# Feed-forward by seven block products in place of eight, in two phases with the gated values in DRAM; bias line written from 128 partitions

## The chip, the cores and the metric

The kernel runs on one core of one Trainium2 chip. A core has a tensor engine for matrix products (PE, with its weight loads PEld), a vector engine (DVE), a scalar engine (ACT), a general engine (POOL) and a queue that issues transfers (SP). The tensor engine writes only into PSUM, here eight banks of 128 partitions by 512 float32. The metric is the device time of one execution in microseconds; lower is better.

## The reference, cut to what matters

One decoder layer on 1024 tokens of 1024 features. The first half is a projection, three groups of attention (sliding window with a relative bias, forgetting attention, latent attention), an output projection, a norm and a residual. The second half is the feed-forward:

```
h = rmsnorm(x, ffn_pre_norm)
u = causal_depthwise_conv(h @ w_up, conv_w, conv_b)      # 5632 columns, 3 taps along the tokens
gate, up = split(u, 2)                                   # 2816 each
y = (gelu(gate) * up) @ w_down
x = x + rmsnorm(y, ffn_post_norm)
```

The relative bias that the sliding window needs is a line of 384 values for each of 8 heads; every query row reads it shifted by one, so it is kept in DRAM once for each of 128 rows.

## The kernel before, in words

Everything is float32. A matrix product is taken as three matmuls of rounded parts: high by high, low by high, high by low (`mm3`, lines 154 to 157). The high part is a rounding copy (`copy_hi`), the low part a subtraction (`sub`).

**Feed-forward.** The 5632 columns of `w_up` are 44 tiles of 128: tile i below 22 is gate, tile 22+i is the up column that belongs to it. `up(i, c)` (line 849) computes one tile for one half c of the tokens: 8 blocks of 128 features by three matmuls of 512 columns, 24 matmuls into one PSUM bank. Bias and the last tap are one ACT instruction that reads the bank (line 861); the other two taps are DVE instructions that also read the bank (line 863), with a two-column `edge` kept for the seam of the halves. Then come gelu, the product gate by up, and the two parts `guh` and `gul`, which stay in SBUF. `down(grp, ...)` (line 1000) multiplies a group of three (at last four) finished tiles by their rows of `w_down`: per block of 128 tokens and half of the columns 9 (12) matmuls into one bank, added by DVE into `yacc`. `fsteps2` (line 56) interleaves: six up tiles, one group of down, and so on. In the last group, each block of tokens is normed, added to the residual `x2d` and stored.

**Weights** are loaded and split by `w_ahead` in the order of the list `wkeys`, four ahead for the load and two for the split; an up tile's split is a cast and a subtraction on DVE, a down tile's is on ACT and POOL (`ENG`, line 38).

**Room.** Nearly all tiles of SBUF come from one pool of 43 slots of 4 KB per partition (`S`, line 95). PSUM has three tags: `mm` and `tp` of two banks each, `sc` of two pairs of banks.

**Bias line.** `bias_line` (line 650) is the filler step `BL` of `FORDER`, late in the dense attention: one small matmul, one DVE addition, and one transfer that writes the 8 rows, each repeated 128 times, from 8 partitions to `bd` in DRAM (1.5 MB). `make_bias` (step `MB`) reads it back.

**Order.** Instructions are written in the order of the program; a scheduler then sets the order of each engine's queue. Each engine runs its queue strictly in that order and waits on semaphores; all transfers are issued by SP, in order.

Of the kernel before, what the change touches and what calls it, by code (L numbers as in the profile page):

```python
# [9 lines left out]
F32 = mybir.dt.float32  # L10
# [3 lines left out]
ALU = mybir.AluOpType  # L14
# [14 lines left out]
          "VAa VAb A2a BL SV A1a A1b A0a A0b A3a A3b MB A2b")  # L29
# [14 lines left out]
GROUPS = (3,) * 6 + (4,)  # L44
# [6 lines left out]
       "F13": 12.11}  # L51
REL = {"Q": -0.965, "A0": 0.595, "A1": 0.092, "M10": 2.221, "B0": 1.243, "M11": 0.739, "O1": 2.446, "B1": 1.525,
       "M20": 2.627, "M21": 1.902, "O0": 2.761, "P": 3.706, "X": 1.747}


def fsteps2():

    s = []
    i0 = 0
    for n in GROUPS:  # L60
        i1 = i0 + n
        for i in range(i0 + 1, i1):
            s += [("up", (i,)), ("up", (NC2 + i,))]
        if i1 < NC2:
            s.append(("up", (i1,)))
        s.append(("dn", tuple(range(i0, i1))))
        if i1 < NC2:
            s.append(("up", (NC2 + i1,)))
        i0 = i1
    return s  # L70
# [3 lines left out]
def trunk_kernel(ctx: ExitStack, tc: tile.TileContext, a: dict, out: bass.AP):  # L74
# [11 lines left out]
    def E(k):  # L86
        return {"A": A, "V": V, "G": G}[ENG[k]]
# [7 lines left out]
    def S(name, dt=F32, shape=(P, 1024), tag="s", bufs=None):  # L95
        return slots.tile(list(shape), dt, tag=tag, name=name, bufs=bufs)

    def sm(name, w, dt=F32):
        return small.tile([P, w], dt, tag=f"sm{w}", name=name)

    def bank(name, tag="mm", shape=(P, 512)):
        tag = TAGS.get(name, tag)
        return (ps2 if tag == "sc" else ps1).tile(list(shape), F32, tag=tag, name=name)
# [4 lines left out]
    def load(dst, src):  # L108
        dst = dst.bitcast(F32) if dst.dtype == F32R else dst
        src = src.bitcast(F32) if src.dtype == F32R else src  # L110
        nc.sync.dma_start(out=dst, in_=src)

    def const(name, shape, src, dt=F32):
        t = cst.tile(list(shape), dt, name=name)
        load(t, src)
        return t

    def blk(i, n=P):
        return slice(i * n, (i + 1) * n)
# [24 lines left out]
    def copy_hi(dst, src, eng):  # L144
        if eng is V:
            V.tensor_copy(dst, src)  # L146
        else:
            A.copy(dst, src)  # L148

    def sub(dst, x, hi, eng=None):  # L150

        (eng or G).tensor_tensor(out=dst, in0=x, in1=hi.bitcast(F32), op=ALU.subtract)  # L152
# [26 lines left out]
    wkeys.append((("up", 0), a["w_up"][0], 1024))  # L179
    wkeys.append((("up", NC2), a["w_up"][NC2], 1024))  # L180
    for key, i in fsteps2():
        wkeys += [((key, j), a["w_up" if key == "up" else "w_down"][j], 1024) for j in i]
# [107 lines left out]
    bd = dram.tile([8, P, 384], F32, name="bd")  # L290
    x2d = dram.tile([SEQ, D], F32, name="x2d")

    def step(f, *x):
        return lambda: f(*x)
# [76 lines left out]
    for t in range(6, NT):  # L371
        tg1(t)
        if t == 6:
            triu = S("triu")
            load(triu[:, 0:P], a["triu"])
    identb = const("identb", [P, P], a["identb"], BF16)
# [273 lines left out]
    def bias_line():  # L650
        rb = sm("rb", 8)
        load(rb[0:32], a["rel_bias"])
        ol = S("oh")
        load(ol[0:32, 0:384], a["ohl"])
        ml = S("ml")
        load(ml[0:8, 0:384], a["mline"])
        ps = bank("bps", "tp")
        T.matmul(ps[0:8, 0:384], lhsT=rb[0:32], rhs=ol[0:32, 0:384], start=True, stop=True)
        V.tensor_tensor(out=ml[0:8, 0:384], in0=ps[0:8, 0:384], in1=ml[0:8, 0:384], op=ALU.add)
        load(bd, ml[0:8, 0:384].rearrange("p (o u) -> p o u", o=1).broadcast_to([8, P, 384]))  # L660

    def make_bias():

        base = bd[0:1, 0:1, 0:1]
        for g in range(2):
            bias[g] = S(f"bias{g}", F32, (P, 4, 256))
            load(bias[g], bass.AP(tensor=base.tensor, offset=base.offset + 4 * g * P * 384 + 127,
                                  ap=[[383, P], [P * 384, 4], [1, 256]]))
# [178 lines left out]
    gu, ut = {}, {}  # L847
    edge = cst.tile([P, 2 * NC2, 2], F32, name="edge")

    def up(i, c, alt=False):  # L850

        wh, wl = W(("up", i))
        ps = bank("psv") if alt else banks("psu", (P, 512))
        for k in range(NK):
            mm3(ps, wh[:, blk(k)], wl[:, blk(k)], h2h[c, k // 2][:, k % 2], h2l[c, k // 2][:, k % 2], k == 0, k == NK - 1)
        if c == 0:
            ut[i] = S("u")
        u = ut[i]
        w = cw[:, i]
        b0 = 512 * c  # L860
        A.activation(u[:, b0:b0 + 512], ps, AF.Identity, bias=w[:, 3:4], scale=w[:, 2:3])  # L861
        for d in (1, 2):
            V.scalar_tensor_tensor(out=u[:, b0 + d:b0 + 512], in0=ps[:, 0:512 - d], scalar=w[:, 2 - d:3 - d],  # L863
                                   in1=u[:, b0 + d:b0 + 512], op0=ALU.mult, op1=ALU.add)
        if c == 0:
            V.tensor_copy(edge[:, i], ps[:, 510:512])  # L866
        else:
            for d in (1, 2):
                V.scalar_tensor_tensor(out=u[:, 512:512 + d], in0=edge[:, i, 2 - d:2], scalar=w[:, 2 - d:3 - d],
                                       in1=u[:, 512:512 + d], op0=ALU.mult, op1=ALU.add)  # L870
        halves = i % NC2 == NC2 - 1
        if c == 0 and not halves:
            return
        cs = blk(c, 512) if halves else slice(0, 1024)
        if i < NC2:
            A.activation(u[:, cs], u[:, cs], AF.Gelu_apprx_tanh)
        else:
            if i - NC2 not in gu:
                gu[i - NC2] = (S("guh", F32R), S("gul", F32R))
            gt = ut[i - NC2]  # L880
            hi, lo = gu[i - NC2]
            V.tensor_tensor(out=u[:, cs], in0=gt[:, cs], in1=u[:, cs], op=ALU.mult)  # L882
            copy_hi(hi[:, cs], u[:, cs], E("guh"))
            sub(lo[:, cs], u[:, cs], hi[:, cs], V if halves else G)


    def fill_ct(i, c):
# [3 lines left out]
        if CKV <= i < KF1:  # L891
# [5 lines left out]
              "BL": (0.6, bias_line), "MB": (0.1, make_bias)}  # L897
# [64 lines left out]
    def swa_a(n, g):  # L962
# [6 lines left out]
             **{f"F{c}{j}": step(up, i, c, j % 2 == 1 and c == 1) for c in range(2) for j, i in enumerate(PRE)}}  # L969
    for j in range(8):  # L970
        steps[f"w{j}"] = step(w_ahead, wo_i + min(8, j + 3), wo_i + j + 1)
# [21 lines left out]

    yacc = {}

    def up_tile(i):
        up(i, 0)
        up(i, 1)

    def down(grp, first, final):  # L1000
        w = [W(("dn", i)) for i in grp]
        if final:
            gff = S("gff")
            load(gff, a["post"][1:2, :].broadcast_to([P, D]))
        for t in range(NT):
            ends = (512, 768, 1024) if final and t == NT - 1 else (512, 1024)
            if first:
                yacc[t] = S(f"y{t}")
            y = yacc[t]
            if final:  # L1010
                sq = sm(f"ysq{len(ends)}", len(ends))
                xt = S("x2r")
                load(xt, x2d[blk(t), :])
            for c, e in enumerate(ends):
                hs = slice(ends[c - 1] if c else 0, e)
                ps = bank("psd", "mm" if c % 2 else "tp")[:, 0:hs.stop - hs.start]
                for x, i in enumerate(grp):
                    mm3(ps, gu[i][0][:, blk(t)], gu[i][1][:, blk(t)], w[x][0][:, hs], w[x][1][:, hs],
                        x == 0, x == len(grp) - 1)
                if first:  # L1020
                    A.copy(y[:, hs], ps)
                else:
                    V.tensor_tensor(out=y[:, hs], in0=ps, in1=y[:, hs], op=ALU.add)  # L1023
                if final:
                    square_sum(sq[:, c:c + 1], y[:, hs])
                    (V if t == NT - 1 and c else G).tensor_tensor(out=y[:, hs], in0=y[:, hs], in1=gff[:, hs], op=ALU.mult)
            if final:
                s, r = sm("zs", 1), sm("zr", 1)
                V.tensor_reduce(out=s, in_=sq, axis=AX.X, op=ALU.add)
                rstd(r, s, D)  # L1030
                for hf in range(2):
                    hs = blk(hf, 512)
                    V.scalar_tensor_tensor(out=y[:, hs], in0=y[:, hs], scalar=r, in1=xt[:, hs], op0=ALU.mult, op1=ALU.add)  # L1033
                    if t == NT - 1:
                        load(out[0, blk(t), hs], y[:, hs])
                if t < NT - 1:
                    load(out[0, blk(t), :], y)

    for key, i in fsteps2():
        if key == "dn":  # L1040
            down(i, i[0] == 0, i[-1] == NC2 - 1)
        elif i[0] not in PRE:
            up_tile(i[0])
# [83 lines left out]
```

## Time and profile before

| | us |
|---|---|
| median of three runs | 1297.54 (1295.29 to 1299.85) |
| the profiled execution, own time | 1293.17 |
| its span, first to last instruction | 1291.3 |
| feed-forward's matmuls in the trace | 546 to 1279 |

The profiled execution lies 4.4 us under the median of the runs, and 1.9 us of its time lie outside the span. Of the span PE is busy 94%, DVE 57%, ACT 34%, POOL 26%. A busy PE is one with at least one matmul in its pipeline; the rate at which matmuls follow each other is read from their starts.

### The profile page before, as it was taken

The page shows a single profiled execution, that of the slowest core. Times are in us where ns is not written, and L with a number is a line of the kernel's source. Part 1 is how long each engine was busy: PE and PEld are TensorE (multiplying, and loading weights), DVE is VectorE, ACT ScalarE, POOL GpSimd, SP SyncE. Part 2 cuts the span into 40 slices and gives each one's busy share as a digit, 9 for nine tenths or more (in the row PEclk, how much of TensorE's full clock was granted, in tenths as well). Part 3 has the DMA queues.
Part 4 walks back from the last instruction along what each step waited for, and adds up shares of the span by engine and source line. Part 5 has one row for each costly group of instructions (what it writes and reads, how often), then busy time and mean ns, then how long its engine had stood idle before and what let it go on. Part 6 is the DMA issues. An engine that isn't in the chain of part 4 may idle for free.

```text
span 1291.3 us, 15510 instructions
## 1 busy us (share of the span) xinstructions
PE 1217.1 (94%) x5978; PEld 1009.6 (78%) x5978; DVE 738.7 (57%) x1214; ACT 443.7 (34%) x919; POOL 337.4 (26%) x204
## 2 busy tenths in 40 slices
PE   8999999839987999999999999999999999999996
PEld 6978887728776878887887887888888888888885
DVE  6346757414789888747416437436446536535566
ACT  6325623303577777523322202202302202202232
POOL 2223322132685354101301301301301300300254
PEclk9999999959999999999999999999999999999998
DMA  9443345232921221312011111201201202202142
GB/s 336 152 134 76 85 146 179 32 65 71 259 67 49 66 82 66 115 65 82 17 49 43 56 35 48 65 33 49 66 14 55 63 16 65 66 17 65 47 182 98
DMA packets 46146, 105.85 MB, mean 82 GB/s; under 512 B 4577, under 2 KB 21513, under 8 KB 46073
## 3 DMA queue, kind: packets, MB, share of 16 engines
q1 hardware_dynamic: 46072, 104.87, 26.7%
q8 instruction: 47, 0.77, 0.2%
q14 instruction: 27, 0.21, 0.1%
HBM read 83.49 MB, written 20.32 MB: 80 GB/s over the span
## 4 chain that ended last, share of the span: by engine, by line
PE 49%; DVE 12%; issue 2%; ACT 2%; POOL 1%; DVEq 0%; POOLq 0%; ACTq 0%
PE psu L155 9%; PE psu L157 9%; PE psu L156 8%; PE psd L155 5%; PE psd L157 5%; PE psd L156 5%; DVE wh L146 4%; DVE u L863 2%; PE pso L155 2%; PE pso L157 2%; PE pso L156 2%; DVE wl L152 1%; DVE y L1033 1%; DVE u L882 1%; ACT u L861 1%
## 5 line engine op out<-in xcount | busy, mean ns | idle before, releaser
L155 PE MATMUL psu<-h2h,wh 128*128 128x512 f32 x688 | 269.8, 392 | 6.0 <-DVE edge L866 6.0
L156 PE MATMUL psu<-h2l,wh 128*128 128x512 f32 x688 | 268.6, 390 | 0.0
L157 PE MATMUL psu<-h2h,wl 128*128 128x512 f32 x688 | 268.5, 390 | 0.0
L863 DVE SCALAR_TENSOR_TENSOR u<-psu,cw,u 128x511 f32<-128x511 f32 (+1 forms) x172 | 128.0, 744 | 176.5 <-ACT u L861 175.7
L152 POOL TENSOR_TENSOR gul<-u,guh 128x1024 fp32r<-128x1024 f32 x21 | 57.2, 2725 | 561.9 <-ACT guh L148 561.9
L861 ACT ACTIVATE u<-psu,cw 128x512 f32<-128x512 f32 x86 | 67.1, 780 | 377.5 <-PE psu L157 227.2
L155 PEld LDWEIGHTS psu<-h2h,wh 128*128 128x128 f32 x688 | 129.6, 188 | 37.6 <-issue 11.1
L157 PEld LDWEIGHTS psu<-h2h,wl 128*128 128x128 f32 x688 | 129.4, 188 | 26.8
L156 PEld LDWEIGHTS psu<-h2l,wh 128*128 128x128 f32 x688 | 129.6, 188 | 26.4
L152 POOL TENSOR_TENSOR wl<-wraw,wh 128x1024 fp32r<-128x1024 f32 (+1 forms) x47 | 110.8, 2370 | 114.0 <-issue 38.5
L156 PE MATMUL psd<-wl,guh 128*128 128x512 f32 (+1 forms) x356 | 137.6, 387 | 0.0
L157 PE MATMUL psd<-wh,gul 128*128 128x512 f32 (+1 forms) x356 | 137.6, 387 | 0.0
L155 PE MATMUL psd<-wh,guh 128*128 128x512 f32 (+1 forms) x356 | 133.7, 387 | 0.0
L1023 DVE TENSOR_TENSOR y<-psd,y 128x512 f32<-128x512 f32 (+1 forms) x97 | 64.6, 682 | 103.6 <-PE psd L157 103.6
L155 PE MATMUL psct<-hTh,wh 128*128 128x512 f32 x176 | 70.8, 402 | 25.6 <-DVE ct L275 25.6
L146 DVE CAST wh<-wraw 128x1024 fp32r<-128x1024 f32 (+2 forms) x65 | 78.8, 1212 | 26.3 <-PE psu L157 13.7
L156 PEld LDWEIGHTS psd<-wl,guh 128*128 128x128 f32 x356 | 66.9, 188 | 13.6
L157 PEld LDWEIGHTS psd<-wh,gul 128*128 128x128 f32 x356 | 66.9, 188 | 13.6
L155 PEld LDWEIGHTS psd<-wh,guh 128*128 128x128 f32 x356 | 66.9, 188 | 13.5
L152 DVE TENSOR_TENSOR wl<-wraw,wh 128x1024 fp32r<-128x1024 f32 (+1 forms) x48 | 58.7, 1223 | 31.5 <-PE psd L156 30.5
L622 ACT ACTIVATE pd<-scd,nm 128x128 f32<-128x128 f32 (+3 forms) x64 | 47.5, 743 | 64.8 <-DVE nm L620 51.8
L156 PE MATMUL psct<-hTl,wh 128*128 128x512 f32 x176 | 69.7, 396 | 0.0
(232 smaller groups left out, 2173.5 us busy)
## 6 DMA issues: line engine op xcount, KB each, us to landing
wraw<-in_w_up_dram SPq DMA_DIRECT2D x44, 512.0 KB
wraw<-in_w_down_dram SPq DMA_DIRECT2D x22, 512.0 KB
wraw<-in_wqk_dram SPq DMA_DIRECT2D x11, 512.0 KB
cd<-ct SPq DMA_DIRECT2D x9, 512.0 KB
xt<-in_x_dram SPq DMA_DIRECT2D x8, 512.0 KB
wraw<-in_w_out_dram SPq DMA_DIRECT2D x8, 512.0 KB
sqr<-cd SPq DMA_DIRECT2D x16, 256.0 KB
xr<-in_x_dram SPq DMA_DIRECT2D x8, 512.0 KB
```

The costliest lines, as they stand in the source:

```text
L146: V.tensor_copy(dst, src)
L152: (eng or G).tensor_tensor(out=dst, in0=x, in1=hi.bitcast(F32), op=ALU.subtract)
L155: T.matmul(ps, lhsT=lh, rhs=rh, start=start, stop=False)
L156: T.matmul(ps, lhsT=lh, rhs=rl, start=False, stop=False)
L157: T.matmul(ps, lhsT=ll, rhs=rh, start=False, stop=stop)
L622: A.activation(p[:, 0:n], s, AF.Exp, bias=nm, accum_out=den[:, i, hd["d"]:hd["d"] + 1])
L861: A.activation(u[:, b0:b0 + 512], ps, AF.Identity, bias=w[:, 3:4], scale=w[:, 2:3])
L863: V.scalar_tensor_tensor(out=u[:, b0 + d:b0 + 512], in0=ps[:, 0:512 - d], scalar=w[:, 2 - d:3 - d], in1=u[:, b0 + d:b0 + 512], op0=ALU.mul ...
L882: V.tensor_tensor(out=u[:, cs], in0=gt[:, cs], in1=u[:, cs], op=ALU.mult)
L1023: V.tensor_tensor(out=y[:, hs], in0=ps, in1=y[:, hs], op=ALU.add)
L1033: V.scalar_tensor_tensor(out=y[:, hs], in0=y[:, hs], scalar=r, in1=xt[:, hs], op0=ALU.mult, op1=ALU.add)
```

## The change

**Products.** A matrix cut into two by two blocks can be multiplied with seven block products in place of eight, if sums and differences of the blocks are formed before and after (the variant of Winograd). For up, the blocks are the gate and the up tile by halves of the features, and the two halves of the tokens: a *pair* j (gate tile j and up tile 22+j) is seven products of 4 x 3 = 12 matmuls, 84 in place of 96. Pairs 0 and 1 stay as they were. `up_prep(j)` forms four sums of weight blocks on POOL and splits seven blocks of 512 columns (ACT rounds, DVE subtracts); `up_pair(j)` runs the products P1 to P7 and combines them; `h2_forms` makes the sums of the activations once. `conv_gate(j)` then runs the three taps over all 1024 tokens from SBUF (tile `C`) instead of PSUM, gelu and the product, and stores the result to `gd` in DRAM.

**Phases.** When all pairs are done, down runs in four chunks of 2, 3, 3 and 3 pairs of row blocks: for each chunk and each of seven products, all forms are made from `gd` and `w_down`, and four blocks of tokens are multiplied, 6 or 9 matmuls each. Seven accumulators a block are kept over the chunks and combined in the last.

**Bias line.** It is made before the attention: the line goes to DRAM once (`bd0`, 12 KB), is read back onto all 128 partitions in four pieces, and each piece is written to `bd`.

```diff
-GROUPS = (3,) * 6 + (4,)
+CHUNKS = (2, 3, 3, 3)
+def bias_line():
...
+        load(bd0, ml[0:8, 0:384])
+        flat = bd0.rearrange("h u -> (h u)").rearrange("(o n) -> o n", o=1)
+        for j in range(4):
+            t = S("bl", F32, (P, 768), tag="p", bufs=4)
+            load(t, flat[:, blk(j, 768)].broadcast_to([P, 768]))
+            load(bd[:, blk(j, 768)], t)
...
-        load(bd, ml[0:8, 0:384].rearrange("p (o u) -> p o u", o=1).broadcast_to([8, P, 384]))
...
+    def conv_gate(j):
+        us = []
+        for i in (j, NC2 + j):
+            cc, u, w = ct2.pop(i), S("u"), cw[:, i]
+            A.activation(u, cc, AF.Identity, bias=w[:, 3:4], scale=w[:, 2:3])
             for d in (1, 2):
+                V.scalar_tensor_tensor(out=u[:, d:], in0=cc[:, 0:SEQ - d], scalar=w[:, 2 - d:3 - d], in1=u[:, d:],
+                                       op0=ALU.mult, op1=ALU.add)
+            us.append(u)
+        A.activation(us[0], us[0], AF.Gelu_apprx_tanh)
+        V.tensor_tensor(out=us[1], in0=us[0], in1=us[1], op=ALU.mult)
+        load(gd[j], us[1])
...
+    def split(x, eng=None):
+        f = S("wf", F32R, (P, 2, 512))
+        A.copy(f[:, 0], x)
+        sub(f[:, 1], x, f[:, 0], eng or V)
+        return f
...
+    def up_prep(j):
...
+        tt(G, s1, a21, a22, ALU.add)
+        tt(G, s3, a11, a21, ALU.subtract)
+        f["A11"] = split(a11)
+        f["A12"] = split(a12)
+        tt(G, a21, s1, a11, ALU.subtract)
+        f["S2"] = split(a21)
+        f["S1"] = split(s1)
+        f["S3"] = split(s3)
+        tt(G, a12, a12, a21, ALU.subtract)
+        f["S4"] = split(a12)
+        f["A22"] = split(a22)
...
+        A.copy(s1, prod("P1"))
+        tt(V, cg[:, lo], prod("P2"), s1, ALU.add)
+        tt(V, u2, prod("P6"), s1, ALU.add)
+        A.copy(s5, prod("P5"))
+        tt(V, u3, prod("P7"), u2, ALU.add)
+        tt(G, cu[:, hi_], u3, s5, ALU.add)
+        tt(G, s5, u2, s5, ALU.add)
+        tt(V, cg[:, hi_], prod("P3"), s5, ALU.add)
+        tt(V, cu[:, lo], prod("P4"), u3, ALU.add)
+        conv_gate(j)
...
+                elif n == "P2":
+                    ts, tb = S("sf"), S("sf")
+                    env2[p] = (ts, tb)
+                    tt(G, ts[:, lo], q("A21"), q("A22"), ALU.add)
...
+        fs = ready.pop((c, n))
+        for t in range(4):
+            ps = bank("dm", "mm") if nb % 3 == 0 else bank("dt", "tp") if nb % 3 == 1 else banks("ds", (P, 512))
+            nb += 1
+            for e, (fa, fb) in enumerate(fs):
+                mm3(ps, fa[:, 0, blk(t)], fa[:, 1, blk(t)], fb[:, 0], fb[:, 1], e == 0, e == len(fs) - 1)
+            take(ps, n, t)
+            if lastc:
+                combine(n, t)
```

What the scheduler makes of it is shown at three places; numbers behind a name are buffer numbers. First SP's queue in the dense attention, in the kernel before (`oh` and `ml` are constants of the bias line, `in_w_out_dram` the weights of the output projection):

```order
L111 DMA mkr<-mkd 64x1024
L111 DMA mkr<-krd 64x1024
L111 DMA mqr<-mqd 128x1024
L111 DMA oh<-in_ohl_dram 32x384
L111 DMA ml<-in_mline_dram 8x384
L111 DMA bd<-ml 1024x1x384
L111 DMA wraw<-in_w_out_dram 128x1024 x2
L111 DMA cd<-ct_2444 128x1024
```

and in the changed kernel, at the same place and then where the bias line now stands, ahead of the first attention head:

```order
L95 DMA wraw<-in_wqk_dram 128x1024 x2
L95 DMA mkr<-mkd 64x1024
L95 DMA mkr<-krd 64x1024
L95 DMA mqr<-mqd 128x1024
L95 DMA wraw<-in_w_out_dram 128x1024 x2
L95 DMA cd<-ct_2457 128x1024
```

```order
L95 DMA bd_110<-ml 8x384
L95 DMA bl<-bd_110 128x768 x4
L95 DMA wraw<-in_wqk_dram 128x1024
L95 DMA bd<-bl 128x768
L95 DMA fqd<-fr 32x128
```

The write of `bd` has left the place ahead of the output projection's weights; in its stead five transfers and four writes stand far ahead of it.

Second, DVE in the feed-forward. The kernel before, from the second tap of a gate tile's first half to the split of weights:

```order
L863 SCALAR_TENSOR_TENSOR u<-psu,cw,u 128x510
L866 COPY edge<-psu 128x2
L863 SCALAR_TENSOR_TENSOR u<-psu,cw,u 128x511
L869 SCALAR_TENSOR_TENSOR u<-edge,cw,u 128x1
L863 SCALAR_TENSOR_TENSOR u<-psu,cw,u 128x510
L869 SCALAR_TENSOR_TENSOR u<-edge,cw,u 128x2
L882 TENSOR_TENSOR u<-u 128x1024
L146 CAST wh<-wraw 128x1024
L152 TENSOR_TENSOR wl<-wraw,wh 128x1024
```

The changed kernel, from the last block of pair 11 (`p_7284` is its P3) to the first blocks of pair 12 (`p_7371` is its P2, `xz` its P6):

```order
L872 TENSOR_TENSOR C<-p_7284,sq_7212 128x512
L859 SCALAR_TENSOR_TENSOR u<-C,cw,u 128x1023 x2
L859 SCALAR_TENSOR_TENSOR u<-C,cw,u 128x1022
L136 TENSOR_TENSOR wf<-wraw,wf 128x512 x2
L859 SCALAR_TENSOR_TENSOR u<-C,cw,u 128x1022
L136 TENSOR_TENSOR wf<-wraw,wf 128x512
L136 TENSOR_TENSOR wf<-sf,wf 128x512 x2
L863 TENSOR_TENSOR u<-u 128x1024
L136 TENSOR_TENSOR wf<-wraw,wf 128x512 x2
L872 TENSOR_TENSOR C<-p_7371,sq_7355 128x512
L872 TENSOR_TENSOR sq_7355<-xz,sq_7355 128x512
```

The taps of pair 11, the splits for pair 13 and the product of gate and up now stand between the last block of one pair and the first of the next, and the taps read SBUF (`C`) instead of PSUM (`psu`).

Third, ACT and PE in the same stretch. ACT in the kernel before:

```order
L876 ACTIVATE u<-u 128x1024
L861 ACTIVATE u<-psu,cw 128x512 x2
L148 CAST guh<-u 128x1024
L148 CAST wh<-wraw 128x1024
L861 ACTIVATE u<-psu,cw 128x512
```

ACT in the changed kernel, from the copy of pair 11's P5 (`sq_7212<-xz`) to that of pair 12's:

```order
L959 COPY sq_7212<-xz 128x512
L857 ACTIVATE u<-C,cw 128x1024 x2
L902 CAST wf<-wraw 128x512 x3
L902 CAST wf<-sf 128x512 x2
L862 ACTIVATE u<-u 128x1024
L902 CAST wf<-wraw 128x512 x2
L956 COPY sq_7355<-p_7357 128x512
L959 COPY sq_7356<-xz 128x512
```

and PE in the changed kernel, at the end of pair 12's P2 (`p2_7371`; `xz_7241` holds pair 11's P6 and P5):

```order
L139 MATMUL p2_7371<-h2h_5321,wf_7189 128x512
L140 MATMUL p2_7371<-h2l_5322,wf_7189 128x512
L141 MATMUL p2_7371<-h2h_5321,wf_7189 128x512
L139 MATMUL xz_7241<-hTf_5655,wf_7052 128x512
L140 MATMUL xz_7241<-hTf_5656,wf_7052 128x512
```

The copy of pair 12's P1 (`p_7357`) stands on ACT behind everything of pair 11 that follows its P5, and pair 11's P5 stands on PE behind pair 12's P1 and P2.

## Rows read from the trace of the kernel before

**Rows 1.** The page: span, engines, busy tenths of PE in 40 slices.
```profile
span 1291.3 us, 15510 instructions
...
PE 1217.1 (94%) x5978; PEld 1009.6 (78%) x5978; DVE 738.7 (57%) x1214; ACT 443.7 (34%) x919; POOL 337.4 (26%) x204
...
PE   8999999839987999999999999999999999999996
```

**Rows 2.** Windows: stretch, length, busy by engine (instructions), granted clock, DMA share, GB/s.
```profile
0.00:100.00 100.00, 90.78 (x490) 76.73 (x491) 48.07 (x108) 40.76 (x85) 24.74 (x25) 1.00 0.62 207
...
546.00:1279.00 733.00, 727.02 (x3212) 598.32 (x3210) 383.17 (x554) 163.63 (x216) 135.34 (x65) 1.00 0.17 56
```

**Rows 3.** Windows around the bias line, same columns.
```profile
270.00:280.00 10.00, 0.00 (x0) 0.00 (x0) 0.60 (x1) 0.00 (x0) 2.98 (x2) 0.50 0.42 84
280.00:290.00 10.00, 9.86 (x43) 8.22 (x44) 4.76 (x9) 2.29 (x5) 7.36 (x3) 0.78 0.05 18
```

**Rows 4.** Timeline there, SP, POOL, PE: start, length, instruction, [idle before <- releaser].
```profile
243.45 0.82 SPq L111 DMA_DIRECT2D bd<-ml  x1
244.38 14.49 SPq L111 DMA_DIRECT2D wraw<-in_w_out_dram  x2
...
277.02 2.34 POOL L152 TENSOR_TENSOR wl<-wraw,wh 128x1024 fp32r<-128x1024 f32 x1 [33.87 <-issue]
...
280.14 0.79 PE L155 MATMUL psct<-hTh,wh 128*128 128x512 f32 x1 [25.56 <-DVE ct L275]
```

**Rows 5.** Timeline of PE in an up tile: first and last of 35 matmuls.
```profile
699.69 0.39 PE L156 MATMUL psu<-h2l,wh 128*128 128x512 f32 x1
...
707.40 0.39 PE L157 MATMUL psu<-h2h,wl 128*128 128x512 f32 x1
```

**Rows 6.** Groups by line and form: count | busy, mean ns | idle before.
```profile
L1023 DVE TENSOR_TENSOR y<-psd,y 128x512 f32<-128x512 f32 x95 | 63.8, 688 | 103.6 <-PE psd L157 103.6
...
L152 DVE TENSOR_TENSOR gul<-u,guh 128x512 fp32r<-128x512 f32 x2 | 1.4, 693 | 1.4 <-ACT guh L148 1.4
...
L821 DVE SCALAR_TENSOR_TENSOR z<-z,zr,gpost 128x1024 f32<-128x1024 f32 x8 | 10.3, 1281 | 2.8 <-POOL zr L126 2.8
...
L148 ACT CAST guh<-u 128x512 fp32r<-128x512 f32 x2 | 1.2, 620 | 7.2 <-DVE u L882 7.2
...
L861 ACT ACTIVATE u<-psu,cw 128x512 f32<-128x512 f32 x84 | 65.5, 780 | 370.6 <-PE psu L157 220.2 <-PE psd L156 150.3
...
L876 ACT ACTIVATE u<-u 128x1024 f32<-128x1024 f32 x21 | 22.3, 1061 | 59.6 <-DVE u L869 59.6
```

**Rows 7.** Timeline of DVE and POOL where they meet.
```profile
876.86 1.23 DVE L152 TENSOR_TENSOR wl<-wraw,wh 128x1024 fp32r<-128x1024 f32 x1
878.00 2.89 DVE L146 CAST wh<-wraw 128x1024 fp32r<-128x1024 f32 x1
...
877.44 2.90 POOL L152 TENSOR_TENSOR gul<-u,guh 128x1024 fp32r<-128x1024 f32 x1 [44.42 <-ACT guh L148]
...
1238.57 1.95 DVE L869 SCALAR_TENSOR_TENSOR u<-edge,cw,u 128x1 f32<-128x1 f32 x1
...
1253.24 0.68 DVE L1023 TENSOR_TENSOR y<-psd,y 128x512 f32<-128x512 f32 x1
...
1235.73 7.12 POOL L152 TENSOR_TENSOR wl<-wraw,wh 128x1024 fp32r<-128x1024 f32 x3 [11.77 <-ACT wh L148]
1246.55 3.80 POOL L1026 TENSOR_TENSOR y<-y,gff 128x512 f32<-128x512 f32 x3 [3.69 <-ACT junk L133]
...
1253.04 1.43 POOL L1026 TENSOR_TENSOR y<-y,gff 128x512 f32<-128x512 f32 x1
```

**Rows 8.** Windows after a short idle of PE, and that idle in PE's timeline.
```profile
388.00:392.00 4.00, 2.07 (x11) 2.07 (x12) 3.94 (x7) 2.67 (x11) 2.61 (x3) 0.77 0.00 0
392.00:396.00 4.00, 3.23 (x20) 2.91 (x19) 3.23 (x8) 2.66 (x9) 1.24 (x2) 0.81 0.00 0
...
389.93 0.97 PE L635 MATMUL tpd<-ident,pd 128*128 128x128 f32 x4 [2.22 <-DVE pt L152]
```

## What the change will do to the time: the prediction

> **What bounds the kernel now.** The page comes first: PE is busy 94% of the span, and one slice of forty reads 3 [rows 1]. Then the windows by stage: from 546 to 1279 us, the feed-forward, PE is busy 727 of 733 us at full granted clock, while DVE is busy 383, ACT 164 and POOL 135 [rows 2]. Starts in PE's timeline say what "busy" is worth: 34 steps from 699.69 to 707.40 are 0.2268 us a matmul [rows 5]. Up is 44 tiles x 2 x 24 = 2112 matmuls and down 22 x 8 x 2 x 3 = 1056; 3168 x 0.2268 = 718.5 of those 733 us. So the feed-forward is bound by the count of matmuls, and a cut of the count is worth its price until another engine is late. The weak slice is another matter. PE idles 25.56 us until 280.14, behind DVE, behind a POOL split that waited 33.87 us for weights [rows 4]. SP had issued the write of `bd` at 243.45 and those weights right behind it; the transfers move 72 to 84 GB/s in that stretch, and PE comes back at a clock of 0.78 [rows 3, 4].
>
> **What the change does, part by part.**
>
> *Bias line.* The 1.5 MB from 8 partitions leave the place ahead of the weights, so the idle goes: 25.6 us, and 2.2 us of lost work, since a mean of 0.78 over 10 us is 4.4 us at half clock [rows 3, 4]. The new writes leave 128 partitions, ahead of the first head, where the first 100 us move 207 GB/s with PE busy 91% [rows 2]; I charge 0.3 us (bounds 0 and 6, the time of the added 1.2 MB of reads at 207 GB/s). Term: -27.5 (-28 to -22).
>
> *Matmuls.* Twenty pairs at 84 for 96 save 240, down at 11 x 7 x 4 x 3 = 924 for 1056 saves 132: 372 x 0.2268 = 84.4 us, -54.4 in up and -29.9 in down, if PE stays the bound.
>
> *Up, the loop between two pairs.* The order shows that PE isn't free to run ahead. PE takes pair j's P5 behind P1 and P2 of pair j+1. P5's copy on ACT releases two POOL additions, the second releases the last DVE addition into `C`, this the taps (ACT, then DVE); DVE then does four taps and splits for pair j+2; and ACT copies P1 of j+1 only behind its casts, into a slot which the fifth of these splits frees. That copy gives P1 of j+2 its bank. Prices: three products 36 x 0.2268 = 8.16 [rows 5]. An ACT copy of 512 is 0.62, twice 1.24 [rows 6]. A POOL addition of 512 is 3.80 / 3 = 1.27, two 2.54 [rows 7]. The DVE addition is 0.69 [rows 6]. The ACT tap lies between 1.06 (gelu of 1024) and 1.56 (twice the 512 form with scale and bias, 0.78); I take 1.2, nearer the row of equal width [rows 6]. DVE instructions in a row start about 0.09 earlier than their lengths say (1.14 apart at 1.23 [rows 7]): four taps of 1024 at 1.28 - 0.08 = 4.8, five splits at 0.69 - 0.08 = 3.05 [rows 6]. Seven hand-overs at about 0.1 (estimate). Sum 8.16 + 1.24 + 2.54 + 0.69 + 1.2 + 7.85 + 0.7 = **22.4 us a pair**, against 19.05 of matmuls and 96 x 0.2268 = 21.77 before. So even undisturbed the loop is no shorter than a pair was: PE idles 3.3 us in each.
>
> *Up, the shared access.* A POOL subtraction issued at 877.44 took 2.90 where three in a row take 7.12 / 3 = 2.37, since DVE's `wl` ran until about 878.0; then DVE's cast took 2.89. A DVE tap of one column with both inputs in SBUF took 1.95, ending with POOL's second subtraction [rows 7]. So such instructions exclude each other and take turns. An addition out of PSUM (1253.24, 0.68) beside a POOL product was not held [rows 7]. The taps of before read PSUM; now they read SBUF, as do the splits, and POOL has four more additions a pair right behind those two. The first passes under the last addition and ACT's tap; of the second some 0.4 is left when DVE's tap is ready; the third and fourth stop DVE for 1.27 each: 2.9, and 25.3 a pair.
>
> *Up, the clock.* With 25.3 PE idles 6.2 us in one piece. The trace has one such short idle, 2.22 us, and the granted clock then reads 0.77 and 0.81 over 8 us, 3.4 us at the lower level, 1.7 us of work [rows 8]. As P1 and P2 follow the idle at once, this would go into the loop. One case is thin, so I take half: **26.2 a pair** (22.4 to 27.0). Term: 20 x (26.2 - 21.77) = +89 (+12 to +105).
>
> *Down.* PE gives back 29.9. A chunk of three is 252 matmuls, 57.2 us. DVE has 42 splits (25.6) and 28 additions out of PSUM (16.8), 42.4; POOL 24 x 1.27 = 30.5. If every POOL addition stops DVE the chunk takes 72.9, if none does 57.2; 18 of the 24 stand in one burst, so I take the middle, 65: 3 x 7.8 = +23 (0 to +47). At the turn, the first splits of `gd` stand on DVE behind the last pair's taps: from P5 the copy, two POOL additions, addition, tap, four taps, two splits come to 0.62 + 2.54 + 0.69 + 1.2 + 4.8 + 1.2 and hand-overs, 12, with nothing on PE: +12. The second chunk's twelve loads wait for slots that the first chunk frees from its third product on, 21.8 us before its end; 6.3 MB at 207 GB/s are 30 us [rows 2], of which P1 needs half early: +5 (0 to 10). Term: +10 (-18 to +45).
>
> *Ends.* The sums of activations (16 instructions of 1024 on DVE, 8 on POOL) stand under four up tiles, 43.5 us; +3 (0 to 10). The last chunk's combinations and eight norms share DVE and POOL with its splits: 4 x 2.04 us of matmuls a product against about 4 us of DVE and POOL a block, +8 (0 to 15).
>
> **The sum.** -27.5 + 89 + 10 + 3 + 8 = +82. The profiled execution took 1293.2: 1375.7. The median of the runs lies 4.4 above it: **1380 us**.
>
> **Rivals.**
>
> *A, the count decides.* Forms and combinations hide, up takes 19.05 a pair: -54.4, down -29.9 with the turn's 12, bias line -27.5: 1293.2 - 100 = 1193, 1198 as a median. For it: DVE is busy 52% of the feed-forward, POOL 18% [rows 2]. Against it: the loop above is made of rows and is 3.3 us too long. 6%.
>
> *B, faster by one mechanism: the shared access doesn't bite.* Place: taps and splits of the up loop and the splits of down. If POOL's additions fit between DVE's instructions, as those out of PSUM show that they can, a pair is 22.4 (+12), the idle of 3.3 is too short for the clock, down is -29.9 + 17, ends +3: -27.5 + 12 - 13 + 3 = -25, 1272 as a median. It decides below a pair of about 23.6, where these terms cancel. Against it: the 2.89 and the 1.95 [rows 7]. 11%.
>
> *C, DVE and POOL are one engine, but nothing else is.* Were the order no loop, a pair would cost the sum of both: 4 x 1.2 + 7 x 0.61 + 1.14 + 5 x 0.6 = 13.2 on DVE and 6 x 1.27 = 7.6 on POOL, 20.8, so -19; the chunks of three at 72.9, 257 with the first, so +17, and 17 at turn and loads. With ends +11 and bias line -27.5 the sum is -1.5: 1296 as a median, no change. The Trainium skill ("Perfetto Trace Analysis", section on optimizing scalar and DVE operations) warns that the two share a read port, so that moving work from one to the other might not help; the exclusion in [rows 7] agrees, but no row shows DVE and POOL both full over a whole stage. Against C as the whole: the queues' order ties ACT and PE into the loop. 8%.
>
> *D, worse.* The clock falls at every pair and the chunks wait for their loads: above 1430. 8%.
>
> The forecast, 1300 to 1430, keeps 67%.
>
> **How the numbers follow.** The likeliest is the forecast, 1380. The range takes part of B and all of C, 1270 to 1430; it leaves out A, D and B's better half, about 2 in 10. A measurement of this kernel can tell about 0.3% from no change, 4 us. Faster: A, B and a little of the forecast's low edge, 0.18. Same: C, 0.08. Slower: 0.74.
>
> **What would show it.** In the changed profile: no idle of 25 us in the dense attention, else the first term is wrong. In the windows of up, P1 of one pair to P1 of the next: 26 us with PE idle before each P1 and released by ACT's copy of P1; 19 says A, 22 says B. DVE taps of 1024 well over 1.28 and POOL additions well over 1.27 say that the access is shared; a granted clock below 1 there says that the clock joins in. In down, PE waiting for DVE's splits within chunks and for loads at their start. If PE waits for none of these and the kernel is slower, the loop isn't the cause and the prediction is wrong in its reason too.

## The result, and the profile of the changed kernel

The changed kernel takes **1460.59 us** (median of four runs, 1457.42 to 1462.66) against 1296.41 for the kernel before: a ratio of 1.126, 95% interval 1.1225 to 1.1295. The profiled execution has a span of 1460.7 us, 169.4 more than [rows 1]. The forecast was 1380 with a range of 1270 to 1430: the right direction, half the size, and outside the range.

The page of the changed kernel, to be read beside [rows 1]: PE's digits are high until the feed-forward, then stay at 6 and 7, and the granted clock (PEclk, in tenths of full speed) falls with them.

```profile
span 1460.7 us, 15601 instructions
...
PE 1191.6 (82%) x5594; PEld 972.0 (67%) x5594; DVE 945.5 (65%) x1327; ACT 583.7 (40%) x1189; POOL 648.2 (44%) x385
...
PE   8989999998899997477776776677677758999990
...
PEclk9989999999999999688988888789879879999995
```

Its windows (columns as in [rows 2]): a stretch of the dense attention, one of the seven-product loop, the turn from up to down, and what is left after the last matmul.

```profile
200.00:300.00 100.00, 97.05 (x553) 81.91 (x552) 55.78 (x92) 37.13 (x84) 30.08 (x12) 1.00 0.31 100
...
660.00:900.00 240.00, 178.40 (x706) 143.68 (x705) 118.60 (x136) 67.30 (x97) 100.09 (x49) 0.86 0.17 57
...
1173.00:1200.00 27.00, 12.73 (x36) 8.76 (x36) 22.61 (x15) 11.36 (x18) 21.81 (x13) 0.68 0.51 195
...
1427.40:1460.70 33.30, 0.18 (x1) 0.00 (x0) 29.51 (x46) 5.78 (x16) 19.87 (x17) 0.55 0.31 126
```

The idle of [rows 4] is gone: PE is busy 97 of 100 us. In the loop PE is busy 178 of 240 us at a clock of 0.86, while no other engine is busy for half of the time. That is the picture of a chain that goes round, not of a full engine. PE's waits name its last link (engine, line, waited for: total, times, longest):

```profile
PE p L139 <- ACT sq L956: 139.8, 19, 7.7
PE p L139 <- ACT wf L902: 24.0, 1, 24.0
...
PE p L141 <- DVE wf L136: 6.8, 1, 6.8
```

Line 956 is ACT's copy of P1, which frees the bank for the P1 of the next pair: 19 waits, one a pair. The 24.0 and 6.8 stand once, at the first seven-product pair. The timeline of one pair, DVE, POOL, ACT and PE from the taps on, shows how the copy came to be late:

```profile
845.44 4.92 DVE L859 SCALAR_TENSOR_TENSOR u<-C,cw,u 128x1023 f32<-128x1023 f32 x3 [1.36 <-ACT u L857]
850.29 1.28 DVE L136 TENSOR_TENSOR wf<-wraw,wf 128x512 fp32r<-128x512 f32 x2
851.49 1.27 DVE L859 SCALAR_TENSOR_TENSOR u<-C,cw,u 128x1022 f32<-128x1022 f32 x1
...
854.49 1.22 DVE L863 TENSOR_TENSOR u<-u 128x1024 f32<-128x1024 f32 x1
857.51 1.29 DVE L136 TENSOR_TENSOR wf<-wraw,wf 128x512 fp32r<-128x512 f32 x2 [1.80 <-ACT wf L902]
...
851.70 5.12 POOL L872 TENSOR_TENSOR wraw<-wraw 128x512 f32<-128x512 f32 x1 [3.61 <-issue]
...
856.86 1.14 ACT L902 CAST wf<-wraw 128x512 fp32r<-128x512 f32 x2 [5.34 <-POOL wraw L872]
857.90 0.58 ACT L956 COPY sq<-p 128x512 f32<-128x512 f32 x1
...
858.53 0.80 PE L139 MATMUL p<-h2h,wf 128*128 128x512 f32 x1 [7.70 <-ACT sq L956]
859.12 0.63 PE L140 MATMUL p<-h2l,wf 128*128 128x512 f32 x1
859.55 0.63 PE L141 MATMUL p<-h2h,wf 128*128 128x512 f32 x1
```

POOL's subtraction for S4 overwrites A12, so it can't start before DVE has split A12 (851.57). By then DVE runs instruction after instruction until 855.71, and the subtraction, 1.29 us in `ring` below, ends at 856.82. ACT's casts of S4 and A22 wait for it, the copy of P1 stands behind them, and PE behind the copy. PE then starts at the lower clock (granted 0.50 from 858.5 to 863.8, the level of 1.2 GHz): its matmuls come 0.43 us apart instead of 0.2268, twelve in this pair, seven in the next.

### The profile page after: what moved, and what is told of

The parts are those of the page before. It is cut to its first block, busy times and chain, and to the rows that moved or that the text cites. A ratio compares the mean times of both kernels' runs of the same rounds, so it can differ in the third digit from the quotient of the medians.

```text
span 1460.7 us, 15601 instructions
## 1 busy us (share of the span) xinstructions
PE 1191.6 (82%) x5594; PEld 972.0 (67%) x5594; DVE 945.5 (65%) x1327; ACT 583.7 (40%) x1189; POOL 648.2 (44%) x385
## 4 chain that ended last, share of the span: by engine, by line
PE 25%; DVE 16%; POOL 13%; issue 11%; ACT 5%; DMA 0%; DVEq 0%; ACTq 0%; POOLq 0%; SPq 0%
POOL wraw L872 6%; DVE wf L136 6%; PE p L139 3%; DVE u L859 3%; PE p L140 3%; PE p L141 3%; POOL sf L872 2%; POOL sq L872 2%; POOL C L872 2%; ACT u L857 2%; ACT wf L902 2%; PE pso L139 1%; PE pso L141 1%; PE pso L140 1%; DVE y L1162 1%
## 5 line engine op out<-in xcount | busy, mean ns | idle before, releaser
L139 PE MATMUL p<-h2h,wf 128*128 128x512 f32 x240 | 114.0, 475 | 163.8 <-ACT sq L956 139.8
L139 PEld LDWEIGHTS p<-h2h,wf 128*128 128x128 f32 x240 | 55.8, 233 | 184.3 <-ACT sq L956 147.8
L859 DVE SCALAR_TENSOR_TENSOR u<-C,cw,u 128x1023 f32<-128x1023 f32 (+1 forms) x88 | 134.1, 1565 | 27.2 <-ACT u L857 27.2
L136 DVE TENSOR_TENSOR wf<-draw,wf 128x512 fp32r<-128x512 f32 x110 | 122.5, 1159 | 20.2 <-ACT wf L902 19.9
L872 POOL TENSOR_TENSOR wraw<-wraw 128x512 f32<-128x512 f32 x20 | 96.6, 4829 | 73.0 <-issue 50.6
L141 PE MATMUL p<-h2h,wf 128*128 128x512 f32 x240 | 107.8, 450 | 6.8 <-DVE wf L136 6.8
L140 PE MATMUL p<-h2l,wf 128*128 128x512 f32 x240 | 108.5, 452 | 0.0
L872 POOL TENSOR_TENSOR sf<-draw 128x512 f32<-128x512 f32 x44 | 67.8, 1572 | 74.6 <-DVE y L1162 33.6
L902 ACT CAST wf<-draw 128x512 fp32r<-128x512 f32 x110 | 62.6, 619 | 89.2 <-POOL draw L872 38.0
L136 DVE TENSOR_TENSOR wf<-wraw,wf 128x512 fp32r<-128x512 f32 x100 | 69.5, 726 | 32.5 <-ACT wf L902 32.4
L141 PE MATMUL psct<-hTh,wl 128*128 128x512 f32 x176 | 68.8, 391 | 0.0
L141 PEld LDWEIGHTS p<-h2h,wf 128*128 128x128 f32 x240 | 53.9, 225 | 20.8 <-DVE wf L136 7.5
```

The costliest lines, as they stand in the source:

```text
L139: T.matmul(ps, lhsT=lh, rhs=rh, start=start, stop=False)
L140: T.matmul(ps, lhsT=lh, rhs=rl, start=False, stop=False)
L141: T.matmul(ps, lhsT=ll, rhs=rh, start=False, stop=stop)
L859: V.scalar_tensor_tensor(out=u[:, d:], in0=cc[:, 0:SEQ - d], scalar=w[:, 2 - d:3 - d], in1=u[:, d:], op0=ALU.mult, op1=ALU.add)
L872: eng.tensor_tensor(out=out_, in0=x, in1=y, op=op)
L902: A.copy(f[:, 0], x)
```

## The experiments

**The bias line alone: at the place of the change, and at its old place.** `bias_early` is the kernel before with the new `bias_line` ahead of the attention. `bias_late` keeps the step `BL` late in the dense attention and only writes the line from 128 partitions, by the same way through DRAM and in the same layout as the change:

```diff
-        load(bd, ml[0:8, 0:384].rearrange("p (o u) -> p o u", o=1).broadcast_to([8, P, 384]))
+        load(bd0, ml[0:8, 0:384])
+        for j in range(4):
+            t = S("bl", F32, (P, 768), tag="p", bufs=4)
+            load(t, flat[:, blk(j, 768)].broadcast_to([P, 768]))
+            load(bd[:, blk(j, 768)], t)
```

> The kernel before with the new bias line alone, at the place that the change gives it. The prediction's term: the idle of 25.6 us in the dense attention and its clock loss go, 0.3 us is paid at the front: 1296 - 27 = 1269 us. The theory from the changed kernel's trace: the first feed-forward matmul comes 17.9 us earlier there (528.4 for 546.3), since the five small transfers and four writes of 0.4 MB stand ahead of the first head's loads on SP and these come some 6 us later: 1296 - 18 = 1278 us.

> The kernel before with the line written from 128 partitions, but at its old place late in the dense attention. If the 8 partitions alone made the long write, and the front of the program is what took back 9 us: the idle goes and nothing is paid at the front, 1296 - 26 = 1270 us. If instead any transfers ahead of the output projection's weights make POOL and DVE late there: the 1.5 MB written and 1.6 MB read back take some 15 us at 200 GB/s, half of the idle stays: 1283 us.

Measured: 1274.96 us, ratio 0.9849 (0.9823 to 0.9876), and 1267.5 us, 0.9792 (0.9765 to 0.9819). First `bias_early`, then `bias_late`: ACT's first cast for the first attention head, and the first 100 us.

```profile
86.86 1.05 ACT L148 CAST fq<-fqr 128x1024 fp32r<-128x1024 f32 x1 [16.43 <-DMA fqr<-cd]
...
0.00:100.00 100.00, 87.70 (x449) 72.58 (x450) 40.41 (x99) 34.82 (x72) 21.27 (x23) 0.96 0.66 225
```

```profile
79.80 1.05 ACT L148 CAST fq<-fqr 128x1024 fp32r<-128x1024 f32 x1 [10.30 <-DMA fqr<-cd]
...
0.00:100.00 100.00, 91.08 (x474) 77.53 (x475) 46.91 (x106) 40.15 (x84) 23.75 (x24) 0.97 0.62 207
```

The place where the line is written, in the kernel before and then in `bias_late`:

```profile
246.00:266.00 20.00, 8.58 (x49) 6.81 (x47) 3.21 (x5) 3.44 (x9) 0.00 (x0) 0.78 0.56 77
```

```profile
246.00:266.00 20.00, 19.25 (x107) 15.81 (x107) 10.15 (x17) 7.39 (x16) 9.97 (x4) 1.00 0.64 212
```

So the way of writing from 8 partitions made the long write: the transfers there move 212 GB/s in place of 77, and PE goes on. Partitions and layout changed together, and in `bias_late` the first load of the output projection's weights has come ahead of the line's copies on SP, so these aren't told apart. The new place costs 7 us at the front: the first head's loads stand on SP behind the line's transfers, 7 us later, with 25 matmuls fewer in the first 100 us.

**The link S4 taken out.** `s4_tile` writes the subtraction into a tile of its own, right behind S2, so that it waits for no split.

```diff
+        s4 = S("s4")[:, 0:512]
+        tt(G, s4, a12, a21, ALU.subtract)
...
-        tt(G, a12, a12, a21, ALU.subtract)
-        f["S4"] = split(a12)
+        f["S4"] = split(s4)
```

> The changed kernel, with the form S4 written into a tile of its own right behind S2 instead of over A12, so POOL need not wait until DVE has read A12 and then until DVE's run of splits ends (5.12 us). Theory of the closing link: in the loop of up ACT's copy of P1 stands behind the casts of S4 and A22, and these wait for this subtraction; then the copy comes as soon as S3's split frees its slot, 3.4 us earlier: 25.5 us a pair for 28.9, 1460 - 65 = 1395 us. Rival, DVE and POOL are full through their shared access and any order gives the same: 28.9 a pair, 1460 us.

Measured: 1424.01 us, ratio 1.1002 (1.0974 to 1.103), half of the expected gain; a pair takes 27.3 us. DVE's splits of S1 and S3, POOL's subtraction, ACT's last cast and the copy, and PE's wait in this pair and the one before:

```profile
865.30 1.28 DVE L136 TENSOR_TENSOR wf<-sf,wf 128x512 fp32r<-128x512 f32 x2
...
859.14 2.16 POOL L872 TENSOR_TENSOR s<-wraw 128x512 f32<-128x512 f32 x1
...
864.19 0.61 ACT L902 CAST wf<-wraw 128x512 fp32r<-128x512 f32 x1
866.62 0.58 ACT L957 COPY sq<-p 128x512 f32<-128x512 f32 x1 [1.82 <-DVE wf L136]
...
839.92 0.80 PE L139 MATMUL p<-h2h,wf 128*128 128x512 f32 x1 [5.45 <-ACT sq L957]
...
867.26 0.80 PE L139 MATMUL p<-h2h,wf 128*128 128x512 f32 x1 [5.45 <-ACT sq L957]
```

The casts are done at 864.80, and the copy waits 1.82 us more, for the split of S3, which frees its slot: the link that the prediction had named stood right behind the one that it had missed.

**The loop opened, and a control.** `ring` takes both scratch tiles of a pair from the ring of four that `C` uses, so that P1's copy needs no slot; `ring_q` takes only the second.

```diff
-        s, q = S("sq1"), S("sq2")
+        s, q = S("sq1", tag="p", bufs=4), S("sq2", tag="p", bufs=4)
```

> The changed kernel, with the two scratch tiles of a pair taken from the ring of four that C uses, so that the copy of P1 needs no slot that a split must free; the order then puts this copy ahead of the taps and casts on ACT, and P5 of a pair at the end of the same pair on PE. If the loop over ACT's queue and the slots is what makes a pair long: no idle of 7.7 us per pair, the clock stays full, a pair takes 19.1 to 22 us, 20 as a middle: 1460 - 20 x 8.9 = 1282 us (1282 to 1320). If DVE and POOL together bound the pair (they are busy 14.3 and 12.0 us of 28.9): 26 us a pair, 1400 us. If the slots don't matter: 1460 us.

> The changed kernel with only the second scratch tile (for P5) taken from the ring of C; the first (for P1) stays in the slots. Room in the slots is then as in the run with both less one, but the orders of ACT and PE stay those of the changed kernel: the copy of P1 behind the casts of S4 and A22, P5 behind P1 and P2 of the next pair. If that order is the cause: 28.9 us a pair as in the changed kernel, 1460 us. If a shortage of slots as such is the cause: some 24 us a pair, 1360 us.

Measured: `ring` 1276.56 us, ratio 0.987 (0.9832 to 0.9909); `ring_q` 1453.63, 1.1228 (1.1186 to 1.1271). In `ring` the scheduler puts the copy of P1 ahead of taps and casts, and P5 at the end of its own pair. The loop's window, the subtraction for S4, the DVE addition and the tap beside it, and ACT's copies of P5 of two pairs:

```profile
660.00:900.00 240.00, 240.00 (x1060) 198.80 (x1059) 187.22 (x216) 107.27 (x151) 98.40 (x77) 1.00 0.25 86
...
752.67 1.29 POOL L872 TENSOR_TENSOR wraw<-wraw 128x512 f32<-128x512 f32 x1 [4.82 <-DVE wf L136]
...
752.45 0.68 DVE L872 TENSOR_TENSOR sq<-xz,sq 128x512 f32<-128x512 f32 x1
753.05 1.99 DVE L859 SCALAR_TENSOR_TENSOR u<-C,cw,u 128x1022 f32<-128x1022 f32 x1
...
759.68 0.59 ACT L959 COPY sq<-xz 128x512 f32<-128x512 f32 x1 [1.57 <-PE xz L141]
...
778.72 0.59 ACT L959 COPY sq<-xz 128x512 f32<-128x512 f32 x1 [1.58 <-PE xz L141]
```

A pair takes 19.04 us, the count of its matmuls (84 x 0.2268 = 19.05): PE never stands and the clock is 1.00. `ring_q` has one slot more than the changed kernel but its orders, and its waits: a slot more isn't enough. What `ring` adds is that P1's copy needs none, and with it comes the new order; these two come together and weren't told apart. The work is the same in all three. In `ring` DVE is still held (a tap of 1.99 us), POOL's subtraction no longer; DVE and POOL are busy 187.2 + 98.4 = 285.6 us of 240. Time in which one is held counts as busy too, so this isn't all work; but neither ends last. Against `bias_early`, which has the same bias line (1274.96), `ring` gains nothing yet: what the products save is lost at the loop's start, at the turn and behind the last matmul.

**The start of the loop.** In `ring` PE still stands 23.98 and 6.75 us at the first seven-product pair. `ring_up2` writes that pair's load ahead of the sums and its forms between their two halves; `plain3` (with the late bias line, and the sums written later) computes pair 2 with eight products; `no_sums` leaves the sums out and takes plain halves of the activations for P4 to P7, so its output isn't the reference's. The cut is from `ring_up2`:

```diff
-       "F13": 12.11, "T0": 11.41, "T1": 11.42, "UL2": 11.43, "UP2": 11.97, "UL3": 12.0}
+       "F13": 12.11, "T0": 11.41, "T1": 11.42, "UL2": 11.36, "UP2": 11.415, "UL3": 12.0}
```

> The kernel of the run with the scratch ring, with the load and forms of the first seven-product pair written between the two halves of the sums of activations instead of behind both. PE stands 23.98 us before that pair's P1 and 6.75 us within it, released by a cast on ACT behind the sums' eight casts. If the order on POOL, ACT and DVE is the cause: the first P1 needs only the first casts, some 12 us of the 24 and the 6.8 go, 1276.6 - 19 = 1258 us. If the loads' late start (slots come free only at 572.7 us) is the cause: the idle stays near 20, 1272 us or more.

> The scratch ring and the bias line at its old place, and pair 2 computed with eight products like pairs 0 and 1, between the sums of activations and the first seven-product pair; its 96 matmuls for 84 cost 2.7 us. Early forms moved the idle there without shortening it (23.98 and 6.75 us became six waits), so the sums and forms on DVE and POOL, not their order, should be what PE waits for; then 21.8 us of plain matmuls cover it: about 20 us of the 31 go, 1276.6 - 8 - 20 + 3 = 1251 us. If the sums can't be covered since they share DVE and POOL with the plain pair's taps: 1268 us.

> The kernel of the run with the scratch ring without the sums of the activations: P4 to P7 take the plain halves instead, so the output isn't the reference's, and 16 slots stay free. The prediction charged the sums 3 us (0 to 10), under the cover of four plain tiles. If that cover were there: 1273 us. If the sums are what PE waits for between the plain pairs and the first seven-product pair, whatever the order (early forms and a third plain pair left the wait there): the two waits of 24.0 and 6.8 us and some 4 us of clock go, less 5 us for the first weights' own forms: 1276.6 - 29 = 1248 us.

Measured: 1274.87 us (0.9849, 0.9822 to 0.9877), 1274.33 (0.9848, 0.9822 to 0.9875) and 1244.94 (0.9606, 0.9591 to 0.962). PE's waits of `ring_up2` there, then PE's wait in `plain3`, then in `no_sums`:

```profile
PE p L139 <- ACT sq L956: 7.1, 1, 7.1
PE p L139 <- ACT wf L902: 5.1, 1, 5.1
PE xz L139 <- ACT hTf L892: 2.8, 1, 2.8
PE p L141 <- DVE wf L136: 2.4, 1, 2.4
```

```profile
PE psu L140 <- DVE wh L131: 31.6, 1, 31.6
```

```profile
573.54 0.50 PE L139 MATMUL p<-h2h,wf 128*128 128x512 f32 x1 [1.15 <-ACT wf L891]
```

The sums cost 1276.56 - 1244.94 = 31.6 us, with the 16 slots that they hold. Written earlier, the forms let PE start sooner, and it waits later: 2.8 us for the sums' own splits (`hTf`), and 7.1 for the copy of P1, which stands on ACT behind the gelu of a plain pair, and this on DVE's taps behind those splits. In `plain3` the third plain pair didn't cover the wait, because its weights' cast stood on DVE behind the sums; it takes nearly as long as `ring`, though its late bias line is worth 7.5 us. Whether weights split ahead of the sums would cover it, stays open (not tried). Why the sums are so long is in the timeline of `ring`, DVE and POOL:

```profile
576.01 7.37 DVE L136 TENSOR_TENSOR hTf<-hf,hTf 128x1024 fp32r<-128x1024 f32 x3 [0.34 <-ACT hTf L892]
...
574.55 6.62 POOL L872 TENSOR_TENSOR hf<-h2h,h2l 128x1024 f32<-128x1024 f32 x2
```

Three instructions of about 1.23 us take 7.37, two of 2.39 take 6.62: they take turns.

**The turn from up to down, and the best version.** `ring_dn` writes the first chunk's loads ahead of pairs 19 and 20 (the last is 21); `ring_all` adds `ring_up2` and the late bias line; `plain3_turn` is `plain3` with the loads of the first chunk, and the forms and splits of its first two products, ahead of the last pair; `best` is `ring_all` with those in place of the loads alone. The cut is from `best`, where the loop also moves behind the definitions that it now needs:

```diff
-    for j in range(2, NC2):
-        up_load(j + 2)
-        up_prep(j + 1)
-        up_pair(j)
...
+    for j in range(2, NC2):
+        up_load(j + 2)
+        up_prep(j + 1)
+        if j == 21:
+            for x in range(2):
+                prep_plan(x)
+        up_pair(j)
```

> The kernel of the run with the scratch ring, with the first chunk's eight loads of down written ahead of the last two pairs instead of behind them. PE stands 14.5 us at the turn (980 to 1010 us), with DVE's last four taps at 8.73 us and POOL's eight additions at 15.66 us, all at once. If the loads' late place behind the last store on SP is the cause: the additions and the first splits run in pair 21, 10 us of the idle go, 1276.6 - 10 = 1267 us. If the last pair's own chain from P5 to its taps is the cause (12 us in the prediction): 1275 us.

> Scratch ring, early forms of the first pair, early loads of down, and the bias line at its old place, all together. If each cause is its own, the gains add: 1276.6 - 19 - 10 - 8 = 1240 us, which would be under the kernel before (1294) and under the kernel before with the late bias line (1267.5). If one gives back what another takes: 1255 us or more.

> The same, and the first chunk's loads, forms and splits of down written ahead of the last pair. Early loads alone changed nothing (1276.1 for 1276.6), since POOL's eight additions and DVE's splits still stood behind the last pair's P5 and taps. If that place in the queues is what PE waits for at the turn: its 14.5 us of idle and about 3 us of clock go, and about 14 us of the time against the run without it, 1237 us. If DVE and POOL are too full in the last two pairs: no gain, 1251 us.

> Scratch ring, bias line at its old place from 128 partitions, the first pair's forms between the halves of the sums, and the first chunk's loads, forms and splits of down ahead of the last pair; no third plain pair. From the run with all but the last (1265.2 us), and the 7.4 us which the early forms and splits of down gave beside the third plain pair: 1258 us, under the kernel before with the late bias line (1267.5). If the early forms of down push the last pairs as much as they gain: 1265 us.

Measured: `ring_dn` 1276.14 us (0.986, 0.9834 to 0.9886), no gain over `ring`; `ring_all` 1265.22 (0.978, 0.9756 to 0.9803), not the 1240 of the expected gains (the measured ones, 7.5, 1.7 and 0.4, do add to nearly that); `plain3_turn` 1266.88 (0.9793, 0.9767 to 0.9818), 7.5 under `plain3`, half of what was expected; `best` 1261.33 (0.9732, 0.9706 to 0.9758). In `ring_dn` the data is there early, and POOL's eight additions still start behind the last pair's, beside DVE's taps and splits:

```profile
993.12 14.69 POOL L872 TENSOR_TENSOR sf<-draw 128x512 f32<-128x512 f32 x8
...
995.20 5.92 DVE L859 SCALAR_TENSOR_TENSOR u<-C,cw,u 128x1023 f32<-128x1023 f32 x3 [1.31 <-ACT u L857]
1001.05 3.42 DVE L136 TENSOR_TENSOR wf<-draw,wf 128x512 fp32r<-128x512 f32 x2
```

So the loads weren't the cause; the place in POOL's and DVE's queues accounts for the half that `plain3_turn` won. `best` lies under both kernels. Of its 2.7%, 2.1% are `bias_late`; what the rest of the change adds is 0.6%, and the two intervals all but touch (0.9758 and 0.9765).

## Why the prediction was wrong, step by step

Each stage, from its matmuls in the two profiles:

| stage | forecast | measured | error, us |
|---|---|---|---|
| up to the output projection's last matmul | -27.5 | -17.9 | +9.6 |
| twenty pairs, with the sums ahead of them | 20 x 26.2 + 3 = 527 | 598 | +71 |
| down, with the turn | 239.5 + 10 = 249.5 | 254.4 | +5 |
| after the last matmul | +8 | +21 | +13 |

The sum of errors is 98.6. The feed-forward before, 733 us, was longer than the 718.5 of its matmuls that I counted, while the two plain pairs after it hardly are (47.3 for 43.5): 10.7 back. The rest, 88, is what the profiled execution's 1462.5 lies above the 1375.7 forecast for it, but for 1 us. Of the 71 in the second row some 48 are 18 full pairs at 2.7 us; the other 23 lie at the loop's two ends, with the sums.

- **The loop: right in its kind, short in its size.** PE took P5 behind P1 and P2 of the next pair and waited for the copy of P1, as the order had shown. Forecast 26.2 us a pair (22.4 to 27.0), measured 520.05 / 18 = 28.9 between 628.61 and 1148.66. From P5's end to P1 it took 858.53 - 840.03 = 18.5 us where I had 22.4 - 8.16 + 2.9 = 17.1. The step that failed is the last link before the copy of P1. The prediction let the copy wait for "a slot which the fifth of these splits frees" and put its standing "behind its casts" at nothing; but the casts of S4 and A22 stood there, and I had not followed S4 back to POOL. `s4_tile` shows the link that was forecast right behind it: a path of 16.2 without S4, 2.3 shorter, and a pair only 1.6 shorter, since the clock took more there.
- **The shared access, right in kind, wrong in place and size.** I charged 2.9 us for POOL's additions stopping DVE. The three taps did take 4.92 for 3.6, 1.3 more, but the dear case was the reverse: DVE's run held one POOL subtraction (5.12 us for 1.29, 3.8 more; 4.83 on average over 20 pairs, 1.39 in `ring`). The Trainium skill ("SBUF — State Buffer", section "SBUF: two separate sides") says that DVE with two SBUF inputs and a GpSimd operation that reads SBUF lock each other out for a whole instruction, by who starts first. The trace agrees for single instructions (the tap of 1.99 us behind the subtraction in `ring`), and 5.12 us is longer than any one of them.
- **The clock, mis-sized.** I charged 0.85 us from the one short idle of [rows 8], halved. The stretch from P1 to P5's end took 11.0 and 9.9 us in turn for 8.16, so 2.3 on average. Halving a thin case was the first half of the error, and its whole 1.7 us was still too little. The loss didn't grow with the idle: in `s4_tile`, after idles of 5.45 us, that stretch took 11.0, 2.8 lost, in one pair after another.
- **The sums: +3 (0 to 10) forecast, 31.6 measured, in `ring`.** I put them "under four up tiles, 43.5 us". But the last of the activations is ready only when those tiles are nearly done, at 569.1 us, and PE ran out of them at 575.4, 6 us later. The sums also were costed as if DVE and POOL ran them side by side.
- **The bias line: the long idle went as forecast, but 0.3 was forecast for its new place and 7 to 9 measured.** I took the 207 GB/s of [rows 2] as room left; what counted was the order on SP ahead of the first head's loads. The bound of 6 wasn't far off, but the value should have been near it.
- **Down and the tail.** Down came near its forecast in sum, not in its parts: waits of 13.6 us at the turn for 12, some 16 behind it for the 23 charged within chunks, none seen for loads where 5 was charged; the rest is mostly slower matmuls. So the nearness is luck in part. The tail of 33 us against 12 was under-sized: DVE is busy 29.5 of these 33.3, with combinations and norms. That they had fallen behind its splits is read from the trace and wasn't tested.
- **The rivals.** A, 6%, said that the loop hides everything and a pair takes 19.05: that is what `ring` does, with one line changed, so the "against" (a loop made of rows) held only for the order that the scheduler had chosen. C fell: a pair of 19.04 us is less than its sum of 20.8 for DVE and POOL. The forecast's direction stood on the order, and the order was rightly read; so the direction wasn't luck, but it belongs to this order and not to the seven products.

## What to carry to other kernels

Follow every operand of the instructions that stand ahead of a critical one in an in-order queue, back to the engine that makes it: an in-place result and a scratch tile's slot closed a loop here that cost 184 us and that one line opened. A cover is only worth the time between the moment when the covered work can start and the moment when the cover ends. And when PE has gaps, charge the clock's whole loss after each: here it was 1.7 us after 2.22, 2.8 after 5.45, 2.3 after 7.7 and 2.2 after 25.6 ([rows 3]).

## What the runs showed of the hardware that was not expected

A single POOL subtraction that became ready inside a run of DVE instructions waited for the end of the whole run (5.12 us for 1.29). A row of eight POOL additions that had started first took turns with DVE instead (14.69 us, 1.84 each, beside three taps of 5.92). The subtraction wasn't held so everywhere: it took 5.11 or 5.12 us in 18 of the 20 pairs, but 2.28 and 2.14 in the first two, inside runs as well. In the pair of `ring` above it starts beside an addition that reads PSUM and took 1.29, and the tap behind that addition was held instead. Why it got no turn in the 18 is open.

After equal idles of 7.70 us the tensor engine ran twelve matmuls at the lower clock (1.2 GHz) in one pair and seven in the next, in turn over most of the loop, so that pairs took 29.5 and 28.5 us. After idles of 5.45 us in `s4_tile` it was twelve in one pair after another.
